# A four-layer fp32 trunk on one core: the SSD's row broadcasts, the transposed head outputs and the chain of the closing norm

## The chip, the core and the metric

The kernel runs on one core of one Trainium2 chip. The metric is the device time of one execution in microseconds (us). The engines are the matrix engine (PE, with its weight loads), DVE and POOL (vector work), ACT (scalar functions) and SP, whose queue issues the weight transfers.

## The reference

```python
for layer in range(2):
    h = rms_norm(x, g[0])
    if layer % 2 == 0:   # combined projection, then two mixers
        mix = concat(gla_mixer(...), na_mixer(...)) @ even_w_out
    else:
        mix = concat(ssd_mixer(...), swa_mixer(...)) @ odd_w_out
    x = x + rms_norm(mix, g[1])
    h = rms_norm(x, g[2])
    f = (silu(h @ ffn_w_gate[layer]) * (h @ ffn_w_up[layer])) @ ffn_w_down[layer]
    x = x + rms_norm(f, g[3])
```

There are 256 tokens of width 2048, all in float32. `rms_norm` divides by the root of the mean square and multiplies with a gain per column. The SSD has 16 heads of 64 columns in two groups, run in both directions:

```python
seg  = a_cum[l] - a_cum[m]              # per head, masked to one side
y    = (exp(seg) * (C B^T)) @ (x * dt)  # both directions added
y    = (y + x * d_skip) * silu(z)
out  = rms_norm(y, norm_g)              # over 1024 columns
```

Beside it stands a windowed attention (SWA) of 8 heads.

## The kernel before, in words

Weights stream from memory in halves of 512 KB (`load_half`, SP's queue). Each half is split into a rounded part `whi` (a CAST on ACT, L198) and a rest `wlo` (a subtraction on DVE, L200); each tile of a product then takes three matmuls of 512 columns (L226, L227, L228, here called main matmuls). Two of the FFN's products use the triples at L694 to L696. A program of pieces written by hand fixes the order at the ends of the layers, and a planner with simulated times places the rest.

Small work (convolutions, heads of the mixers) runs as generators beside the main matmuls: `tick` adds `rate` per tile of work, `step` advances the first `width` generators by one yield each. In the odd mixer these are RATE1 and WIDTH1 (L45).

**The end of a layer.** `post` takes the last product in four column blocks n = 0 to 3, for two halves of the tokens t = 0, 1. Each block is added to `f` on DVE (`add`, L444), squared and summed on ACT (`sumsq`, L360), and multiplied in place with the gains `gb` (L484: POOL for n < 2, DVE else), which must wait until ACT has read the block. At n = 3 `rstd` (L345 ff.) adds the four sums (L351), scales them and adds EPS (L355) on DVE, and POOL takes the power -0.5 (L356, result `prs`). Then the string PROG[0] (L54) orders the pieces: X0 to X3 add the four blocks to `x` (L468, DVE), T transposes a block of the new x on PE (L342, four matmuls `tp`), G makes its rounded part on ACT (L385), L the rest on DVE (L389), `p` prepares one half of weights (CAST and `wlo`), `q` issues a held back half of the last products. Capitals are t = 0, small letters t = 1. Pieces are pinned: PE and DVE keep this order. X is also saved to memory from POOL's queue (L1389). In the last layer there is no T; X is written out by SP (the tail).

**The SSD, before.** `ssd_dt` makes the cumulated decays `ac` (48 rows, both directions) and splits them into a rounded part and a rest (`achl`). For each head `ssd` broadcasts the head's two rows to 128 partitions with a matmul with a selecting column (`acb`, L1293), subtracts the transposed decays (`seg`, L1298, DVE, four pieces), takes the exponential on ACT, and multiplies with dt and with C B^T on POOL and DVE (L1305 to L1314 are POOL's). Four matmuls (eight records, 64 columns each) give `yp` with tokens on the partitions (L1320). POOL's x times `dskip` is added, the result is gated with `sz`, squared and summed on ACT; at the end ACT scales y, 16 transposes turn it and `split` makes the two parts for the output product.

Of the kernel before, what the change touches and what calls it, by code (L numbers as in the profile page):

```python
# [44 lines left out]
RATE1, WIDTH1 = .9, 6  # L45
# [8 lines left out]
PROG = ("X0 X1 p X2 p p X3 T0 q G0 T1 q q G1 L0 T2 p L1 p T3 G2 q x0 L2 x1 p G3 x2 x3 L3",  # L54
# [7 lines left out]
           ("alog", (1,)), ("dskip", (16,)), ("sink", (8,)), ("snT", (8,))),  # L62
# [31 lines left out]
class Trunk:  # L94
# [263 lines left out]
    def sumsq(self, src, acc):  # L358
        j = self.junk.tile([P, 512], mybir.dt.bfloat16, tag="junk", name=self.nm("sq"))
        self.nc.scalar.activation(j, src, AF.Square, accum_out=acc)  # L360
# [47 lines left out]
    def post(self, li, gi, nseg, after, f=None, before=None):  # L408
# [7 lines left out]
        rs = [self.small([P, 1], "prs", "prs") for _ in range(2)]  # L416
        state = {"si": 0}
# [7 lines left out]
        def seg(mk, xk):  # L425
# [25 lines left out]
            def run(prog):  # L451

                for c in prog.split():
# [12 lines left out]
                    xs, d = self.x[t][j // 2][:, s2], f[t][j // 2][:, s2]  # L466
# [5 lines left out]
            for n in range(4):  # L472
                def evac(t, ps, n=n):
# [5 lines left out]
                    with self.tc.high_priority(offset=NORM):  # L479
                        d = add(t, ps, n, n == 3)  # L480
                        self.sumsq(d, ssp[t][:, n:n + 1])
                        if n == 3:
                            self.rstd(ssp[t], 4, D, rs[t])
                        i = (nc.gpsimd if n < 2 else nc.vector).tensor_mul(out=d, in0=d, in1=gb[n])  # L484
                        if n == 3:
                            self.pin(i)
# [600 lines left out]
    def odd_mixers(self, norm, after):  # L1087
        nc = self.nc
        self.have = {}
# [24 lines left out]
        ssp = [self.small([P, 2], "yss", "yss") for _ in range(2)]  # L1114
        for g in range(2):
# [4 lines left out]
            xs = self.slot([P, 2, 512], nm="xs")  # L1120
            self.have[f"xs{g}"] = xs
            for c in range(4):
                self.conv(4 * g + c, xt, row, self.conv_end_x(xs, c, f"xs{g}{c}"))
# [51 lines left out]
    def conv_end_x(self, xs, c, key):  # L1175
        nc = self.nc

        def end(y):
            nc.vector.scalar_tensor_tensor(out=y[:, 1], in0=y[:, 1], scalar=1.0, in1=y[:, 0], op0=ALU.add, op1=ALU.mult)
            ps = self.mx([P, 2, P], "xsT")  # L1180
            for t in range(2):
                nc.tensor.transpose(ps[:, t], y[:, 1, t * P:(t + 1) * P], self.ident)
            nc.scalar.mul(xs[:, :, c * P:(c + 1) * P], ps, 0.5)
# [4 lines left out]
    def ssd_dt(self, xu):  # L1188
# [35 lines left out]
        hl = self.slot([P, 2, T], F32R, nm="achl")  # L1224
        zero = self.mtmp([P, 2, T], nm="dz")
        nc.vector.memset(zero, 0.0)
        nc.scalar.copy(hl, zero)
        for d in range(2):
            a = ac[32 * d:32 * d + 16]
            nc.scalar.copy(hl[0:16, d], a)  # L1230
            hb = zero[32 * d:32 * d + 16, 0]
            if d:
                nc.vector.tensor_copy(hb, hl[0:16, d].bitcast(F32))
            else:
                hb = hl[0:16, d].bitcast(F32)
            nc.vector.tensor_sub(hl[32:48, d], a, hb)
# [7 lines left out]
        sel = self.keep.tile([P, 16], F32R, tag="sel", bufs=1, name="sel")  # L1244
        nc.scalar.copy(sel, zero[:, 1, 0:16])
        for d in range(2):
            r = slice(32 * d, 32 * d + 16)
            nc.scalar.copy(sel[r], self.ident[r, r])
        self.have["dt"] = (hl, nat, sel)
        yield  # L1250

# [17 lines left out]
    def ssd(self, g, bc, ssp):  # L1269

        nc = self.nc
        yield from self.need("dt", f"bc{g}0", f"bc{g}1")
        hl, nat, sel = self.have["dt"]
        cb = self.ssd_cb(bc)
        cbf = cb.rearrange("p a b -> p (a b)")
        xs = self.have[f"xs{g}"]
# [4 lines left out]
        for qd in range(2):  # L1281
            yield from self.need(f"xs{g}{2 * qd}", f"xs{g}{2 * qd + 1}")
            cols = slice(256 * qd, 256 * qd + 256)
            xd = self.mtmp([P, 2, 4, 64], nm="xd")
            dk = self.dskip[:, 8 * g + 4 * qd:8 * g + 4 * qd + 4]
            for t in range(2):
                nc.gpsimd.tensor_mul(out=xd[:, t], in0=xs[:, t, cols].rearrange("p (h c) -> p h c", h=4),
                                     in1=dk.unsqueeze(2).broadcast_to([P, 4, 64]))
            yp = self.mx([P, 2, 256], "yp")
            for hq in range(4):  # L1290
                h, hc = 8 * g + 4 * qd + hq, (4 * qd + hq) * 64
                pb = self.mx([P, 2, T], "acb")
                nc.tensor.matmul(pb.rearrange("p a t -> p (a t)"), sel[:, h:h + 1].to_broadcast([P, P]),  # L1293
                                 hl.rearrange("p a t -> p (a t)"), start=True, stop=True)
# [7 lines left out]
                for i, (c0, c1, d, l0, mt) in enumerate(parts):  # L1302
                    r = 32 * d + h
                    if i in PSTT:
                        nc.gpsimd.tensor_scalar(out=s[:, c0:c1], in0=s[:, c0:c1], scalar1=nat[:, 2 + mt, r:r + 1],  # L1305
                                                scalar2=None, op0=ALU.mult)
                        if i == PSTT[-1]:
# [7 lines left out]
                if PY:  # L1315
                    yield
                for lt in range(2):
                    o = yp[:, lt, hq * 64:(hq + 1) * 64]
                    for mt in range(2):
                        nc.tensor.matmul(o, sb[:, lt + 4 * mt], xs[:, mt, hc:hc + 64], start=mt == 0, stop=mt == 1)  # L1320
                yield
            if y is None:
                y = self.slot([P, 2, 512], nm="y")
# [9 lines left out]
    def ssd_out(self, ssp, mix):  # L1333
# [3 lines left out]
        for g in range(2):  # L1337
            self.new_mix(mix, g)
# [147 lines left out]
```

## Time and profile before

| | us |
|---|---|
| three runs | 2190.62, 2187.39, 2187.41 |
| median | 2187.41 |
| profiled execution | 2186.18 |
| its span, first to last instruction | 2184.4 |

The mean clock granted to PE was 0.998 of full speed. The page gives busy times for each engine, DVE 1732.4 us, ACT 1219.6 and POOL 170.7 among them. Rows of a timeline give the start of a group of instructions in us from the span's start, its length, and in brackets the idle time of the engine ahead of it and what ended it. Records of PE overlap: the end of a record is modelled, so distances between starts are read.

### The profile page before, as it was taken

Reading aid. Unit: us, or ns where it says so; the run is one execution under the profiler, and the core shown is the slowest. Engines: PE = TensorE matmul, PEld = TensorE weight load, DVE = VectorE, ACT = ScalarE, POOL = GpSimd, SP = SyncE. Lnnn points to the kernel's source line nnn. Section 1 sums busy time; section 2 is a strip of 40 time slices with the busy share of each in tenths; the row PEclk is TensorE's granted clock in tenths of the full one; section 3 lists DMA queues with packets and bytes.
Section 4 is the critical chain, followed back from the end, with each engine's and each line's share of the span. In section 5 each row is a group of like instructions: output and inputs, shape, how many; then the busy total and the mean of one; then the engine's idle time right before and its main releaser. Section 6 shows DMA issues by size and latency. Waiting matters only on the chain. (4 is left out here: it accounts for less than half of the span.)

```text
span 2184.4 us, 28289 instructions
## 1 busy us (share of the span) xinstructions
PE 2154.6 (99%) x10416; PEld 1801.2 (82%) x10416; DVE 1732.4 (79%) x2208; ACT 1219.6 (56%) x1619; POOL 170.7 (8%) x217
## 2 busy tenths in 40 slices
PE   8999999999999999999999999999999999999997
PEld 7888888788888888888879988778888888888886
DVE  6988655766878898888879997776787889888786
ACT  7645445555565555555556455655556555555653
POOL 0001110100000000000021363210000000000001
PEclk9999999999999999999999999999999999999999
DMA  8444565674675655567466443567466555646644
GB/s 293 147 136 161 191 196 192 198 274 143 201 238 180 206 169 200 190 208 250 159 219 227 155 155 128 200 203 273 147 198 230 192 205 167 213 166 221 242 154 144
DMA packets 117322, 424.49 MB, mean 194 GB/s; under 512 B 13392, under 2 KB 13520, under 8 KB 117184
## 3 DMA queue, kind: packets, MB, share of 16 engines
q1 hardware_dynamic: 110592, 400.61, 54.6%
q0 software_dynamic: 6448, 21.99, 3.0%
q8 instruction: 81, 1.33, 0.2%
q14 instruction: 57, 0.47, 0.1%
q10 hardware_dynamic: 144, 0.10, 0.0%
HBM read 414.25 MB, written 8.39 MB: 193 GB/s over the span
## 5 line engine op out<-in xcount | busy, mean ns | idle before, releaser
L200 DVE TENSOR_TENSOR wlo<-raw,whi 128x1024 fp32r<-128x1024 f32 x608 | 750.1, 1239 | 291.9 <-ACT whi L198 283.2
L198 ACT CAST whi<-raw 128x1024 fp32r<-128x1024 f32 x608 | 639.2, 1054 | 591.7 <-PE acc L228 397.9
L228 PE MATMUL acc<-whi,xt 128*128 128x512 f32 x1760 | 686.9, 391 | 0.0
L227 PE MATMUL acc<-wlo,xt 128*128 128x512 f32 x1760 | 686.0, 391 | 0.2 <-DVE wlo L200 0.2
L226 PE MATMUL acc<-whi,xt 128*128 128x512 f32 x1760 | 675.8, 391 | 1.3 <-ACT xt L385 1.3
L226 PEld LDWEIGHTS acc<-whi,xt 128*128 128x128 f32 x1760 | 330.8, 188 | 69.4 <-ACT xt L385 1.7
L227 PEld LDWEIGHTS acc<-wlo,xt 128*128 128x128 f32 x1760 | 330.8, 188 | 69.2 <-DVE wlo L200 0.7
L228 PEld LDWEIGHTS acc<-whi,xt 128*128 128x128 f32 x1760 | 330.7, 188 | 68.2
L198 ACT CAST whi<-sw 128x1024 fp32r<-128x1024 f32 x252 | 265.7, 1054 | 207.6 <-PE acc L228 141.1
L200 DVE TENSOR_TENSOR wlo<-sw,whi 128x1024 fp32r<-128x1024 f32 x252 | 305.2, 1219 | 55.6 <-ACT whi L198 52.4
L696 PE MATMUL sq<-whi,so 128*128 128x512 f32 x504 | 196.1, 389 | 0.0
L695 PE MATMUL sq<-wlo,so 128*128 128x512 f32 x504 | 196.1, 389 | 0.0
L694 PE MATMUL sq<-whi,so 128*128 128x512 f32 x504 | 195.8, 390 | 0.0
L643 DVE TENSOR_TENSOR sw<-sw,sw 128x1024 f32<-128x1024 f32 x144 | 174.2, 1218 | 14.4 <-DMA sw<-sstream 13.8
L259 PE MATMUL acc<-xt,whi 128*128 128x512 f32 x384 | 136.3, 400 | 0.0
L696 PEld LDWEIGHTS sq<-whi,so 128*128 128x128 f32 x504 | 94.6, 188 | 19.7
L695 PEld LDWEIGHTS sq<-wlo,so 128*128 128x128 f32 x504 | 94.6, 188 | 19.4
L694 PEld LDWEIGHTS sq<-whi,so 128*128 128x128 f32 x504 | 94.6, 188 | 19.4
L262 PE MATMUL acc<-xt,wlo 128*128 128x256 f32 x384 | 105.0, 284 | 0.0
L434 POOL DMA_DIRECT2D gb<-norm_gains x16 | 8.7, 545 | 1196.1 <-issue 1183.1
L226 PE MATMUL acc<-whi,mixh 128*128 128x512 f32 x256 | 98.4, 396 | 0.0
L228 PE MATMUL acc<-whi,mixl 128*128 128x512 f32 x256 | 97.9, 391 | 0.0
(272 smaller groups left out, 2324.4 us busy)
## 6 DMA issues: line engine op xcount, KB each, us to landing
raw<-wstream SPq DMA_DIRECT2D x612, 512.0 KB, 4.9
sw<-sstream SPq DMA_DIRECT2D x144, 512.0 KB, 6.6
gb<-norm_gains POOLq DMA_DIRECT2D x16, 256.0 KB, 4.4
xm<-x POOLq DMA_DIRECT2D x16, 256.0 KB, 4.5
x<-xm POOLq DMA_DIRECT2D x8, 512.0 KB, 5.6
x<-x SPq DMA_DIRECT2D x4, 512.0 KB, 8.5
x<-x POOLq DMA_DIRECT2D x4, 512.0 KB, 5.7
xf<-x POOLq DMA_DIRECT2D x8, 256.0 KB, 3.5
```

The costliest lines, as they stand in the source:

```text
L198: self.pin(nc.scalar.copy(hi, src))
L200: self.pin(nc.vector.tensor_sub(lo, src, hi.bitcast(F32)))
L226: self.pin(nc.tensor.matmul(ps[t], xh, wh[:, k % 2], start=s, stop=False))
L227: self.pin(nc.tensor.matmul(ps[t], xh, wl[:, k % 2], start=False, stop=False))
L228: self.pin(nc.tensor.matmul(ps[t], xl, wh[:, k % 2], start=False, stop=e))
L259: wide = lambda s, e: nc.tensor.matmul(ps, wh[:, kt % 8], self.joined(kt, xt), start=s, stop=e)
L262: nc.tensor.matmul(ps[:, 0], wl[:, kt % 8], xt[0][kt // 4][:, kt % 4, :], start=False, stop=False)
L434: self.tc.keep_in_program_order(nc.gpsimd.dma_start(out=gb[n], in_=self.dr["norm_gains"][li, gi, n * 512:(n + 1) * 512].partition_broadcas ...
L643: nc.vector.tensor_add(a, a, b)
L694: nc.tensor.matmul(ps, xh, wh[:, k], start=s, stop=False)
L695: nc.tensor.matmul(ps, xh, wl[:, k], start=False, stop=False)
L696: nc.tensor.matmul(ps, xl, wh[:, k], start=False, stop=e)
```

## The change

Three things change together.

1. The norm at a layer's end. The squares are scaled, so that their sums add up to the mean. At n = 2 DVE adds the first three sums and EPS; at n = 3 ACT adds the last one itself (Identity with a bias), and POOL takes the power of that. The product with the gains of n = 3 goes to a tile of its own, `pg`, so that it need not wait for the square; that of t = 1, n = 1 moves from POOL to DVE.
2. The order of pieces, PROG[0]: two `p` stand ahead of X2 X3, all four X ahead of T0; L0, G2 and the pieces of t = 1 stand elsewhere. WIDTH1 goes from 6 to 7.
3. The SSD. POOL writes the decays to memory (`acrows`) and reads each pair's rows back to all 128 partitions (512 KB for a pair of heads); the `acb` matmuls, the split of `ac` and the selecting columns go. `yp` is made transposed for a pair of heads: x is the stationary part (64 columns), `seg` streams with 256 columns, and the two heads' outputs lie on partitions 0 to 63 and 64 to 127. The D-skip is one operation on DVE with x transposed; `z` is transposed for the gate (16 transposes); the squares are summed over partitions by matmuls with ones (`yss`); and the factor of the norm is applied from a row that `rstd_rows` spreads.

```diff
-RATE1, WIDTH1 = .9, 6
+RATE1, WIDTH1 = .9, 7
...
-PROG = ("X0 X1 p X2 p p X3 T0 q G0 T1 q q G1 L0 T2 p L1 p T3 G2 q x0 L2 x1 p G3 x2 x3 L3",
+PROG = ("X0 X1 p p X2 X3 p T0 q G0 T1 q q G1 T2 p L0 L1 q p T3 G2 L2 x0 G3 x1 p x2 x3 L3",
...
-        self.nc.scalar.activation(j, src, AF.Square, accum_out=acc)
+        self.nc.scalar.activation(j, src, AF.Square, scale=scale, accum_out=acc)
...
-                    xs, d = self.x[t][j // 2][:, s2], f[t][j // 2][:, s2]
+                    xs, d = self.x[t][j // 2][:, s2], prod[t][j]
...
-                        self.sumsq(d, ssp[t][:, n:n + 1])
+                        self.sumsq(d, ssp[t][:, n:n + 1], D ** -0.5)
+                        if n == 2:
+                            nc.vector.reduce_sum(out=rs[t], in_=ssp[t][:, 0:3], axis=AX.X)
+                            nc.vector.tensor_scalar_add(rs[t], rs[t], EPS)
                         if n == 3:
-                            self.rstd(ssp[t], 4, D, rs[t])
-                        i = (nc.gpsimd if n < 2 else nc.vector).tensor_mul(out=d, in0=d, in1=gb[n])
+                            nc.scalar.activation(ssp[t][:, 3:4], ssp[t][:, 3:4], AF.Identity, bias=rs[t])
+                            nc.gpsimd.tensor_tensor(out=rs[t], in0=ssp[t][:, 3:4], in1=self.mhalf, op=ALU.pow)
+                        p = prod[t][n] = d if n < 3 else self.tmp([P, 512], nm="pg")
+                        i = (nc.gpsimd if n < 2 - t else nc.vector).tensor_mul(out=p, in0=d, in1=gb[n])
...
+        rows = self.dram.tile([16, 2, T], F32, name="acrows")
         for d in range(2):
...
+            nc.gpsimd.dma_start(out=rows[:, d], in_=ac[32 * d:32 * d + 16])
...
+    def ac_rows(self, k):
+
+        if k in self.acs or k > 7:
+            return
+        self.acs[k] = self.slot([P, 2, 2, T], nm="acb")
+        self.tc.keep_in_program_order(self.nc.gpsimd.dma_start(
+            out=self.acs[k], in_=self.have["dt"][0][2 * k:2 * k + 2].partition_broadcast(P)))
...
-            for hq in range(4):
-                h, hc = 8 * g + 4 * qd + hq, (4 * qd + hq) * 64
-                pb = self.mx([P, 2, T], "acb")
-                nc.tensor.matmul(pb.rearrange("p a t -> p (a t)"), sel[:, h:h + 1].to_broadcast([P, P]),
-                                 hl.rearrange("p a t -> p (a t)"), start=True, stop=True)
+        for c in range(4):
+            yield from self.need(f"xs{g}{c}")
+            self.ac_rows(4 * g + c)
+            self.ac_rows(4 * g + c + 1)
+            both = []
+            for i in range(2):
+                h = 8 * g + 2 * c + i
+                pb = self.acs[4 * g + c][:, i]
...
-                if PY:
-                    yield
-                for lt in range(2):
-                    o = yp[:, lt, hq * 64:(hq + 1) * 64]
-                    for mt in range(2):
-                        nc.tensor.matmul(o, sb[:, lt + 4 * mt], xs[:, mt, hc:hc + 64], start=mt == 0, stop=mt == 1)
+                both.append(s)
                 yield
+            if PY:
+                yield
+            yp = self.mx([P, T], "yp")
+            for mt in range(2):
+                for i in range(2):
+                    r = slice(64 * i, 64 * i + 64)
+                    self.turn(nc.tensor.matmul(yp[r], xs[:, mt, c * P + 64 * i:c * P + 64 * i + 64],
+                                               both[i][:, 512 * mt:512 * mt + T], start=mt == 0, stop=mt == 1), i or mt)
+            yield
...
-            nc.vector.tensor_add(y[:, :, cols], yp, xd.rearrange("p t h c -> p t (h c)"))
+            nc.vector.scalar_tensor_tensor(out=y[:, c], in0=xT[:, c], scalar=self.dskip[:, 4 * g + c:4 * g + c + 1],
+                                           in1=yp, op0=ALU.mult, op1=ALU.add)
...
+                    nc.tensor.transpose(tp[:, k, t * P:(t + 1) * P], z[:, t, c:c + P], self.ident)
+            nc.vector.tensor_mul(y[:, cs], y[:, cs], tp)
+            nc.scalar.activation(sq[:, cs], y[:, cs], AF.Square)
...
+        nc.vector.tensor_add(sq[:, 0:2], sq[:, 0:2], sq[:, 2:4])
+        ps = self.mx([P, 2], "yss")
         for t in range(2):
...
+            for c in range(2):
+                nc.tensor.matmul(ps[:, t:t + 1], sq[:, c, t * P:(t + 1) * P], self.ones[:, 0:1], start=c == 0, stop=c == 1)
+        nc.vector.tensor_copy(ssp[:, :, g], ps)
...
+        row = self.rstd_rows(rs)
...
-                nc.scalar.mul(y[:, t], y[:, t], r)
...
-                tp = self.transpose4(self.have[f"y{g}"][:, t])
-                self.split(tp, mix[0][g][:, :, sl], mix[1][g][:, :, sl], self.snT[:, 4 * g:4 * g + 4], self.mtmp)
...
+                    nc.vector.scalar_tensor_tensor(out=y[:, c], in0=y[:, c], scalar=self.snT[:, 4 * g + c:4 * g + c + 1],
+                                                   in1=row, op0=ALU.mult, op1=ALU.mult)
+                nc.scalar.copy(mix[0][g][:, cs], y[:, cs])
+                nc.vector.tensor_sub(mix[1][g][:, cs], y[:, cs], mix[0][g][:, cs].bitcast(F32))
```

The changed kernel's lines stand 1 to 18 lower (X at L469, the product with the gains at L490, Identity at L487, the power at L488, `yp` at L1318).

PE in the odd mixer, before: `yp` of two heads and the broadcasts of two more, between main matmuls.

```order
L228 MATMUL acc_11296<-whi_11495,xt_9664 128x512
L226 MATMUL acc_11296<-whi_11495,xt_9664 128x512
L1320 MATMUL yp_11092<-xs_10152,seg_11095 128x64 x4
L1320 MATMUL yp_10968<-xs_10654,seg_11103 128x64 x4
L1293 MATMUL acb_11198<-achl_10127,sel 128x512
L1293 MATMUL acb_11206<-achl_10127,sel 128x512
L227 MATMUL acc_11296<-wlo_11497,xt_9664 128x512
L228 MATMUL acc_11296<-whi_11495,xt_9664 128x512
```

PE in the odd mixer, after: one pair of heads, its first matmul apart from the other three.

```order
L228 MATMUL acc_11129<-whi_11158,xt_9679 128x512
L1318 MATMUL yp_11207<-seg_11034,xs_10141 64x256
L226 MATMUL acc_11265<-whi_11255,xt_9588 128x512
L227 MATMUL acc_11265<-wlo_11257,xt_9588 128x512
L1318 MATMUL yp_11207<-seg_11118,xs_10141 64x256
L1318 MATMUL yp_11207<-seg_11034,xs_10141 64x256
L1318 MATMUL yp_11207<-seg_11118,xs_10141 64x256
L228 MATMUL acc_11265<-whi_11255,xt_9588 128x512
L226 MATMUL acc_11265<-whi_11255,xt_9588 128x512
```

The broadcasts are gone, and a `yp` row is one matmul of 64 output partitions and 256 columns; of the eight pairs four stand like this one, with main matmuls between, and four stand with their four rows together.

ACT at the end of layer 0's mixer, before (`sq` the squares, `pss_3030` the sums of t = 0).

```order
L198 CAST whi_3773<-raw_3706 128x1024
L360 ACTIVATE sq_3743,pss_3031<-f_3264 128x512
L360 ACTIVATE sq_3778,pss_3030<-f_3348 128x512
L198 CAST whi_3809<-raw_3746 128x1024
L198 CAST whi_3817<-raw_3752 128x1024
L360 ACTIVATE sq_3800,pss_3031<-f_3264 128x512
L385 ACTIVATE xt_3829<-tp_3832,ca 128x128 x4
L198 CAST whi_3823<-raw_3771 128x1024
```

ACT at the same place, after; L487 is the new Identity.

```order
L198 CAST whi_3775<-raw_3706 128x1024
L360 ACTIVATE sq_3745,pss_3031<-f_3264 128x512
L360 ACTIVATE sq_3780,pss_3030<-f_3348 128x512
L198 CAST whi_3809<-raw_3748 128x1024
L487 ACTIVATE pss_3030<-pss_3030,prs_3032 128x1
L198 CAST whi_3815<-raw_3754 128x1024
L360 ACTIVATE sq_3800,pss_3031<-f_3264 128x512
L385 ACTIVATE xt_3829<-tp_3832,ca 128x128 x4
```

The Identity comes behind the last square of t = 0, with one CAST between.

DVE at the same place, before (L444 add, L468 X, L351 and L355 the norm, L200 `wlo`).

```order
L351 TENSOR_REDUCE ss_3780<-pss_3030 128x1
L484 TENSOR_TENSOR f_3348<-f_3348,gb_3612 128x512
L355 TENSOR_SCALAR ms_3782<-ss_3780 128x1
L444 TENSOR_TENSOR f_3264<-f_3264,acc_3786 128x512
L468 SCALAR_TENSOR_TENSOR x_3598<-f_3095,prs_3032,x_3598 128x512 x2
L200 TENSOR_TENSOR wlo_3811<-raw_3746,whi_3809 128x1024
L468 SCALAR_TENSOR_TENSOR x_3600<-f_3348,prs_3032,x_3600 128x512
L200 TENSOR_TENSOR wlo_3819<-raw_3752,whi_3817 128x1024
L200 TENSOR_TENSOR wlo_3825<-raw_3771,whi_3823 128x1024
L468 SCALAR_TENSOR_TENSOR x_3600<-f_3348,prs_3032,x_3600 128x512
L389 SCALAR_TENSOR_TENSOR xt_3829<-tp_3832,ca,xt_3829 128x128 x4
```

DVE at the same place, after (L445 add, L469 X, L490 product with the gains).

```order
L445 TENSOR_TENSOR f_3348<-f_3348,acc_3760 128x512
L490 TENSOR_TENSOR pg_3784<-f_3348,gb_3612 128x512
L445 TENSOR_TENSOR f_3264<-f_3264,acc_3786 128x512
L469 SCALAR_TENSOR_TENSOR x_3598<-f_3095,prs_3032,x_3598 128x512 x2
L200 TENSOR_TENSOR wlo_3811<-raw_3748,whi_3809 128x1024
L200 TENSOR_TENSOR wlo_3817<-raw_3754,whi_3815 128x1024
L469 SCALAR_TENSOR_TENSOR x_3600<-f_3348,prs_3032,x_3600 128x512
L469 SCALAR_TENSOR_TENSOR x_3600<-pg_3784,prs_3032,x_3600 128x512
L490 TENSOR_TENSOR f_3264<-f_3264,gb_3608 128x512
L200 TENSOR_TENSOR wlo_3827<-raw_3773,whi_3825 128x1024
```

The sum and the scaling are gone from here, X2 and X3 stand together behind two `wlo`, and a product that POOL did (`gb_3608`, t = 1) stands behind X3.

## Rows read from the trace of the kernel before

**Rows 1.** the page, part 1: busy time, share of the span, instructions.

```profile
PE 2154.6 (99%) x10416; PEld 1801.2 (82%) x10416; DVE 1732.4 (79%) x2208; ACT 1219.6 (56%) x1619; POOL 170.7 (8%) x217
```

**Rows 2.** PE's waits by line: total us, times, longest us.

```profile
PE tp L342 <- DVE x L468: 5.9, 6, 1.4
...
PE tp L342 <- issue: 3.0, 2, 1.5
PE apo L1062 <- DVE mxv L1031: 1.6, 1, 1.6
...
PE apo L1062 <- ACT pT L1058: 0.8, 1, 0.8
...
PE yp L1320 <- POOL seg L1314: 0.2, 1, 0.2
```

**Rows 3.** PE's timeline: start us, us, engine line op; one `acb` broadcast.

```profile
1319.46 0.40 PE L1293 MATMUL acb<-achl,sel 128*128 128x512 f32 x1
1319.69 0.40 PE L228 MATMUL acc<-whi,xt 128*128 128x512 f32 x1
```

**Rows 4.** PE's timeline: one head's `yp` and the matmuls behind it.

```profile
1387.86 1.00 PE L1320 MATMUL yp<-xs,seg 128*128 128x64 f32 x8
...
1388.98 0.40 PE L228 MATMUL acc<-whi,mixl 128*128 128x512 f32 x1
```

**Rows 5.** PE's timeline: `gs` (split rows), then `as` (256 columns).

```profile
79.34 0.39 PE L259 MATMUL acc<-xt,whi 128*128 128x512 f32 x1
79.66 1.16 PE L895 MATMUL gs<-ge 64*128 64x128 f32 x16
...
80.98 0.39 PE L259 MATMUL acc<-xt,whi 128*128 128x512 f32 x1
...
1361.36 1.02 PE L1029 MATMUL as<-kw,qT 128*128 128x256 f32 x4
...
1362.45 0.40 PE L228 MATMUL acc<-whi,xt 128*128 128x512 f32 x1
```

**Rows 6.** PE's timeline at the end of layer 0's mixer.

```profile
420.56 0.39 PE L228 MATMUL acc<-whi,mixl 128*128 128x512 f32 x1
422.39 0.66 PE L342 MATMUL tp<-ca,x 128*128 128x128 f32 x4 [1.45 <-DVE x L468]
...
429.31 0.66 PE L342 MATMUL tp<-ca,x 128*128 128x128 f32 x4 [1.25 <-DVE x L468]
```

**Rows 7.** DVE's timeline at the same place.

```profile
420.98 0.69 DVE L444 TENSOR_TENSOR f<-f,acc 128x512 f32<-128x512 f32 x1 [0.34 <-PE acc L228]
421.59 1.41 DVE L468 SCALAR_TENSOR_TENSOR x<-f,prs,x 128x512 f32<-128x512 f32 x2
422.91 2.75 DVE L200 TENSOR_TENSOR wlo<-raw,whi 128x1024 fp32r<-128x1024 f32 x1
...
428.52 0.74 DVE L468 SCALAR_TENSOR_TENSOR x<-f,prs,x 128x512 f32<-128x512 f32 x1
```

**Rows 8.** ACT's timeline at the same place.

```profile
419.67 1.03 ACT L198 CAST whi<-raw 128x1024 fp32r<-128x1024 f32 x1
```

**Rows 9.** POOL's timeline at the same place.

```profile
420.72 0.57 POOL L356 TENSOR_TENSOR prs<-ms,mhalf 128x1 f32<-128x1 f32 x1 [1.30 <-DVE ms L355]
...
423.26 1.30 POOL L484 TENSOR_TENSOR f<-f,gb 128x512 f32<-128x512 f32 x1
```

**Rows 10.** DVE's timeline at the end of layer 1's mixer.

```profile
1459.82 1.22 DVE L200 TENSOR_TENSOR wlo<-raw,whi 128x1024 fp32r<-128x1024 f32 x1
```

**Rows 11.** DVE's timeline in the tail, then POOL's.

```profile
2168.36 3.77 DVE L468 SCALAR_TENSOR_TENSOR x<-f,prs,x 128x512 f32<-128x512 f32 x4
...
2177.20 2.74 DVE L468 SCALAR_TENSOR_TENSOR x<-f,prs,x 128x512 f32<-128x512 f32 x4 [0.66 <-POOL prs L356]
...
2169.34 1.57 POOL L484 TENSOR_TENSOR f<-f,gb 128x512 f32<-128x512 f32 x1 [1.29 <-ACT sq L360]
```

**Rows 12.** POOL's groups by line and form: busy us, mean ns.

```profile
L1314 POOL TENSOR_TENSOR seg<-seg 128x256 f32<-128x256 f32 x16 | 20.4, 1282 | 0.6
```

## What the change was predicted to do

> **What bounds the kernel now.** I read the page's list of busy times first: the matrix engine (PE) is busy for 2154.6 of 2184.4 us [rows 1], so time can come only from what PE executes, from the places where it waits, and from the tail after its last matmul. Next the list of PE's waits: little is in it, and the reader should see that it has two families [rows 2]. One is `tp`, the transposes at a layer's end that wait for the new `x`: 5.9 us in six waits on DVE and 3.0 in two put down to issue. The other is the odd mixer: `apo` of the windowed attention on DVE (1.6) and ACT (0.8), `yp` of the SSD on POOL (0.2). Last I read the timelines of the places that the diff touches, PE first, then the engine it waits for. Because PE's records overlap, a price on PE is a distance between starts: one main matmul of 512 columns costs 0.23 [rows 3].
>
> **The change, part by part.** The profiled execution took 2186.2 us, 1.2 less than the median of 2187.4; I make the sum against the first and add 1.2.
>
> *Broadcasts.* The 16 `acb` matmuls leave PE. One costs the distance 1319.46 to 1319.69, 0.23 [rows 3], so -3.7. In their place POOL issues two small writes and eight reads of 512 KB. I cost these at nothing: each read is issued one pair of heads ahead, and the cover is the work of that pair. If the cover is gone, `seg` comes late (third rival).
>
> *Head outputs.* Before, a head costs 1387.86 to 1388.98 less one main matmul, 0.89 [rows 4]; 16 heads, -14.2. After, a pair of heads takes four matmuls, two for each half of the output partitions, eight records of 256 columns. Four such records in `as` cost 1361.36 to 1362.45 less 0.23, 0.86, so 0.215 each [rows 5]. Do two halves run side by side? No row of before splits the output partitions. The nearest are the `gs` records, which split the contraction rows: 16 records of 128 columns, with one L262 of 256 columns (0.115) behind them, fill 79.34 to 80.98 less 0.23, so 1.29 without the L262 [rows 5]. At half of 0.215 each, 16 in a row would be 1.72; eight side by side are 0.86, and 0.43 is left over, which I read as a toll for going into split mode and back. So an undisturbed pair of heads is 4 x 0.215 + 0.43 = 1.29. The order shows four of the eight pairs undisturbed and four with main matmuls between the first half and the other three. For these I add one lone matmul and a second toll, 0.43 + 0.43, giving about 2.15. Sum 4 x 1.29 + 4 x 2.15 = 13.8. The bounds: 8.6 (no toll anywhere, 8 x 0.86 + 4 x 0.43) and 19.0 (nothing side by side: 8 x 1.72, a toll for each of 12 visits).
>
> The Trainium skill (TensorEngine Tiling (Array Packing), Key Properties) speaks against this part: it says that a change of tiling mode drains the engine, which would make the split groups pay twice; the 0.43 above agrees with it. By TensorE: Matmul & The Clock Gate, Part 3, small outputs in different column groups run concurrently, with next to nothing per tile; by that alone the groups would cost the lower bound. No run here shows column halves yet.
>
> *Norm of y.* The 16 transposes of y become 16 of z, same shape: zero. Added are 16 records of one column (`yss`), priced at 0.11 each as `yp`'s 64-column records are (0.89 / 8) [rows 4], 1.8, and four for `rstd_rows`, 0.4. Bounds 1.0 to 2.6. The edits on DVE and ACT (gate, D-skip, the 0.5 folded away, fewer scalings) I cost at nothing, since PE has main matmuls beside them; if that cover fails, it shows as `apo` or `yp` waiting.
>
> PE's work in the SSD thus changes by -3.7 - 14.2 + 13.8 + 2.2 = **-1.9**, between -8.3 and +3.7.
>
> *Waits of the odd mixer.* They hold 2.6 [rows 2]. In the new order 15 main matmuls stand between a transpose `apt` and its `apo`, and `yp` waits only once for a pair. I take 1.0 as left: **-1.6**. Bounds -2.6 and +3 (each pair waits 0.4, as the larger yp gaps of before).
>
> *Layer ends.* Three boundaries share the 8.9 us of `tp` waits [rows 2]; the first (mixer to FFN of layer 0) stands for them. There T0 waits 1.45 and T3 1.25 [rows 6]. Is the first wait shortened? The norm's own chain gets shorter, but on ACT a CAST of 1.03 stands between the last square and the new Identity (the order), as it stood behind the square before [rows 8]; so Identity ends near 420.9 and POOL's pow (0.57 [rows 9]) near 421.5. On DVE the add of the other half stands ahead of X0, till 421.67, and X0 begins at 421.59 now [rows 7]. Both limits hold the first wait where it is. The later ones shrink: before, X2 and X3 stood among three `wlo`, X3 started at 428.52, and one of the `wlo` took 2.75 beside POOL's gain product [rows 7, 9], where one took 1.22 without it [rows 10]. After, that product moves to DVE (0.69, after X3), and X0 X1, two `wlo`, X2 X3 end near 421.6 + 1.4 + 2.4 + 1.4 = 426.8, 2.5 us before T3 could start. The first waits, 3 x 1.47 = 4.4, stay; the other 4.5 I take down to 1.5, because pieces that came early now make the `lo` pieces and `wlo` late: **-3.0**. Bounds -4.5 and 0.
>
> WIDTH1 lets one more background strand advance at once; I cost it at nothing beyond the order already counted. SP's queue of weight loads is the same row for row, and POOL's saves of `xm` come with their X, with one product less ahead of them: nothing.
>
> *Tail.* At the end no CAST stands behind the square. X of the second half of the tokens starts at 2177.20 [rows 11]. Before it, the first half's four X took 3.77, with POOL's product at 2169.34 beside them for 1.57 [rows 11]; without it they take 2.75 as the last four do, 1.0 less; the product moves to DVE, into its idle time before the last add. On the norm's chain the sum, the scale and the gain product no longer stand behind the last square: some 0.8 less on DVE, 0.1 more on ACT. **-1.7**, bounds 0 and -2.5.
>
> Sum: -1.9 - 1.6 - 3.0 - 1.7 = -8.2; 2186.2 - 8.2 + 1.2 = **2179.2 us**.
>
> **Rivals.** 0.2% of the time, 4.4 us, is about what a measurement of this kernel can tell from no change.
>
> *Halves in turn.* If the two column halves don't run side by side, the pairs cost 19.0 in place of 13.8: 2184.4. Against it: the `gs` rows. For it: those split rows, not columns.
>
> *No toll.* If going into column halves costs nothing, 8.6 in place of 13.8: 2174.0. For it: the 0.43 is one sample of a group beside small shapes.
>
> *SSD late, the slower side.* The subtraction that makes `seg` reads its rows from SBUF now, where it read PSUM, and POOL works on `seg` too. POOL's add of 256 columns takes 1.28 on average [rows 12], and the `wlo` of 2.75 shows what DVE and POOL do to each other [rows 7, 9]. If every pair's `yp` waits for one such add, PE loses 8 x 1.28 = 10.2, and the 1.6 of the mixer's waits is not won: 2179.2 + 11.8 = 2191.0. It decides from the point at which a pair's last add ends after PE has come to its `yp`, about one add late at each. Against it: of 16 heads, `yp` waited 0.2 us in all on POOL [rows 2]. The Trainium skill (SBUF — State Buffer, 🔬 SBUF: two separate sides) has this as a rule: DVE in its fast modes from SBUF and POOL share a port pair as a lock, and descriptors of POOL's DMAs wait too. The 2.75 agrees for two SBUF inputs; for the DMA issues no row here decides.
>
> That the change doesn't do what it says can be in one part: the first waits stay, as said, so the norm's shorter chain wins only in the tail. This lies in the forecast.
>
> **How the numbers follow.** Forecast 0.56, halves in turn 0.13, no toll 0.18, SSD late 0.13. The forecast's own bounds on waits and tail are some 4 us each way, 2175 to 2183. The range adds the no-toll case with part of its spread and halves in turn: 2172 to 2187; what it leaves out is SSD late and the far ends. Faster means under 2183.0: no toll, nine tenths of the forecast and a quarter of halves in turn, 0.71. Slower is over 2191.8: under half of SSD late and nothing else of weight, so with its doubled form 0.08. The rest, 0.21, is the same.
>
> **What would show it.** Right: `yp` pairs at 1.3 undisturbed and 2.1 split; no `acb` on PE; the first `tp` wait near 1.5 at each boundary and the later ones near 0.5; X of the second half near 2175.5. Wrong: `yp` or DVE's `seg` waiting for POOL or for a DMA at most pairs, pairs of 1.7 or more undisturbed, a first `tp` wait under 1 us, or new waits of main matmuls for `wlo` at the boundaries.

## The result, and the profile after

The changed kernel takes 2174.74 us (median of six runs, 2174.09 to 2176.83) against 2187.4 for the kernel before in the same comparison: the ratio is 0.9941, with a 95% interval of 0.9928 to 0.9954. It is 12.7 us faster, where 8.2 were forecast; 2179.2 was said and the range was 2172 to 2187. The profiled execution took 2174.74 with a span of 2172.9.

The page's busy times and PE's list of waits, of the changed kernel:

```profile
PE 2151.1 (99%) x10356; PEld 1790.2 (82%) x10356; DVE 1729.1 (80%) x2223; ACT 1216.7 (56%) x1613; POOL 169.5 (8%) x215
```

```profile
PE tp L342 <- DMA ca<-ca: 5.1, 1, 5.1
PE tp L342 <- issue: 3.0, 2, 1.5
PE tp L342 <- DVE x L469: 1.4, 1, 1.4
PE acc L226 <- ACT xt L385: 1.4, 1, 1.4
PE acc L228 <- DVE xt L389: 0.4, 2, 0.2
```

Against [rows 1, 2] the reader should see that PE's busy time fell by only 3.5 us; most of the gain is in waits. Of the `tp` waits at the layer ends only the three first ones are left (3.0 + 1.4; the 5.1 for `ca` stood there before as well, 5.2), and `apo` and `yp` no longer appear in the list at all.

The main matmuls are the same 9320 records in both traces, so the place where time is won can be read from their starts: the k-th one after less the k-th one before, the change from one place to the next.

| stretch | before, from to | won in the two traces | forecast |
|---|---|---|---|
| layer 0's mixer | 0 to 420 | -0.6 | 0 |
| its end | 420 to 500 | 1.4 | 1.0 |
| FFN 0 | 500 to 1131 | 0.3 | 0 |
| FFN 0's end | 1131 to 1200 | 1.4 | 1.0 |
| odd mixer | 1200 to 1440 | 6.8 | 3.5 |
| its end | 1456 to 1490 | 0.9 | 1.0 |
| tail, behind the start of the last main matmul | 2172.8 to 2184.4 | 1.2 | 1.7 |

Together the two traces differ by 11.4; the medians differ by 12.7, because the profiled execution before lies 1.2 under its median. (The 0.6 in layer 0, where nothing is changed, is of the size by which single executions differ there; the profiled executions of two experiments, product on POOL and late head first, stood some 3 us behind the changed kernel there, with a wait of `gs` for DVE.)

PE's timeline of the changed kernel, an undisturbed pair of heads and then a split one:

```profile
1294.01 0.39 PE L226 MATMUL acc<-whi,xt 128*128 128x512 f32 x1
1294.33 1.08 PE L1318 MATMUL yp<-seg,xs 128*64 128x256 f32 x8
1295.34 0.50 PE L227 MATMUL acc<-wlo,xt 128*128 128x512 f32 x1
1295.68 0.40 PE L228 MATMUL acc<-whi,xt 128*128 128x512 f32 x1
```

```profile
1269.46 0.39 PE L228 MATMUL acc<-whi,xt 128*128 128x512 f32 x1
1269.78 0.65 PE L1318 MATMUL yp<-seg,xs 128*64 128x256 f32 x2
1270.35 0.50 PE L226 MATMUL acc<-whi,xt 128*128 128x512 f32 x1
1270.69 0.40 PE L227 MATMUL acc<-wlo,xt 128*128 128x512 f32 x1
1271.02 1.08 PE L1318 MATMUL yp<-seg,xs 128*64 128x256 f32 x6
1272.02 0.50 PE L228 MATMUL acc<-whi,xt 128*128 128x512 f32 x1
1272.36 0.40 PE L226 MATMUL acc<-whi,xt 128*128 128x512 f32 x1
```

With the main matmuls around them taken off (two of 0.227 each time), the undisturbed pair costs 1.22 (1294.01 to 1295.68), a lone first matmul 0.78 (1269.46 to 1270.69), and the three others 1.22. Before, two heads cost 1.78 [rows 4].

DVE's, ACT's and POOL's timelines at the end of layer 0's mixer, after:

```profile
421.57 0.69 DVE L445 TENSOR_TENSOR f<-f,acc 128x512 f32<-128x512 f32 x1 [1.02 <-PE acc L228]
422.18 1.41 DVE L469 SCALAR_TENSOR_TENSOR x<-f,prs,x 128x512 f32<-128x512 f32 x2
423.50 2.36 DVE L200 TENSOR_TENSOR wlo<-raw,whi 128x1024 fp32r<-128x1024 f32 x2
425.77 0.74 DVE L469 SCALAR_TENSOR_TENSOR x<-f,prs,x 128x512 f32<-128x512 f32 x1
426.44 0.74 DVE L469 SCALAR_TENSOR_TENSOR x<-pg,prs,x 128x512 f32<-128x512 f32 x1
```

```profile
420.27 1.03 ACT L198 CAST whi<-raw 128x1024 fp32r<-128x1024 f32 x1
421.20 0.29 ACT L487 ACTIVATE pss<-pss,prs 128x1 f32<-128x1 f32 x1
```

```profile
421.57 0.57 POOL L488 TENSOR_TENSOR prs<-pss,mhalf 128x1 f32<-128x1 f32 x1 [1.56 <-ACT pss L487]
```

Identity stands behind a CAST, the power ends at 422.14, the add ends at 422.26, and X0 starts at 422.18: both limits are there, as forecast from [rows 7 to 9]. The two `wlo` take 2.36 together where one took 2.75 beside POOL's product [rows 7], and X3 ends at 427.2 in place of 429.3.

The tail, DVE:

```profile
2165.44 2.08 DVE L469 SCALAR_TENSOR_TENSOR x<-f,prs,x 128x512 f32<-128x512 f32 x3 [1.08 <-POOL prs L488]
```

The X of the second half of the tokens start 2.9 us behind the last main matmul's start (2162.53), where they started 4.4 behind it before [rows 11].

### The profile page after: what moved, and what is told of

The parts are those of the page before. It is cut to its first block, busy times and chain, and to the rows that moved or that the text cites. A ratio compares the mean times of both kernels' runs of the same rounds, so it can differ in the third digit from the quotient of the medians.

```text
span 2172.9 us, 28179 instructions
## 1 busy us (share of the span) xinstructions
PE 2151.1 (99%) x10356; PEld 1790.2 (82%) x10356; DVE 1729.1 (80%) x2223; ACT 1216.7 (56%) x1613; POOL 169.5 (8%) x215
## 4 chain that ended last, share of the span: by engine, by line
PE 78%; issue 1%; DVE 1%; POOL 0%; ACT 0%; POOLq 0%; DVEq 0%; ACTq 0%
PE acc L228 19%; PE acc L227 19%; PE acc L226 18%; PE sq L701 5%; PE sq L700 5%; PE sq L702 5%; PE tp L342 1%; PE accb L299 1%; PE accb L300 1%; PE accb L301 1%; PE yp L1318 0%; DVE x L469 0%; PE apo L1068 0%; PE as L1035 0%; PE accl L280 0%
## 5 line engine op out<-in xcount | busy, mean ns | idle before, releaser
L200 DVE TENSOR_TENSOR wlo<-raw,whi 128x1024 fp32r<-128x1024 f32 x608 | 745.3, 1232 | 288.6 <-ACT whi L198 280.2
L200 DVE TENSOR_TENSOR wlo<-sw,whi 128x1024 fp32r<-128x1024 f32 x252 | 305.4, 1221 | 55.6 <-ACT whi L198 52.6
```

The source lines that it names most:

```text
L200: self.pin(nc.vector.tensor_sub(lo, src, hi.bitcast(F32)))
```

## The experiments

Each run is named, with its median of five runs or more; the changed kernel's is 2174.74, and that of the kernel before was 2187.27, 2187.60 and 2186.96 in the three comparisons.

### The layer ends

**Old pieces** (2177.78, 2177.25 to 2178.89).

```diff
-PROG = ("X0 X1 p p X2 X3 p T0 q G0 T1 q q G1 T2 p L0 L1 q p T3 G2 L2 x0 G3 x1 p x2 x3 L3",
+PROG = ("X0 X1 p X2 p p X3 T0 q G0 T1 q q G1 L0 T2 p L1 p T3 G2 q x0 L2 x1 p G3 x2 x3 L3",
```

> The changed kernel with the old order of pieces at the layer ends (PROG[0]), all else as changed. Theory A: the order carries most of what the layer ends won (some 4 us in the traces), so 2.5 to 3.5 us slower than the changed kernel, about 2177.7, and T3 waits near 1 us again. Rival B: the norm's chain and the product taken from POOL carry it; then within 0.7 us of the changed kernel, about 2175.2.

3.0 slower, as theory A has it: later `tp` waits return at all three ends (`tp` on DVE 7.1 us in seven waits). The order of the pieces is worth 3.0 beside the new norm.

**Old norm** (2180.94, 2179.44 to 2181.04).

```diff
-                            nc.scalar.activation(ssp[t][:, 3:4], ssp[t][:, 3:4], AF.Identity, bias=rs[t])
-                            nc.gpsimd.tensor_tensor(out=rs[t], in0=ssp[t][:, 3:4], in1=self.mhalf, op=ALU.pow)
-                        p = prod[t][n] = d if n < 3 else self.tmp([P, 512], nm="pg")
-                        i = (nc.gpsimd if n < 2 - t else nc.vector).tensor_mul(out=p, in0=d, in1=gb[n])
+                            self.rstd(ssp[t], 4, D, rs[t])
+                        i = (nc.gpsimd if n < 2 else nc.vector).tensor_mul(out=d, in0=d, in1=gb[n])
```

> The changed kernel with the old norm at the layer ends (sum, scale and gain product of the last block in the chain, POOL's product at t = 1), the new order of pieces kept. Theory A: the first waits stay near 1.6 each, the tail is 1.3 longer and the layer ends lose under 1 us, so about 2176.7. Rival B: the shorter chain is what lets X2 and X3 end early; then 3 us or more slower, 2178 and up, with new waits of tp at all three ends.

6.2 slower, so theory A is wrong in size and B right about it; but B's waits of `tp` are not there. DVE's and PE's timelines at the end of layer 0's mixer, of this run:

```profile
424.18 3.88 DVE L200 TENSOR_TENSOR wlo<-raw,whi 128x1024 fp32r<-128x1024 f32 x2
427.99 1.40 DVE L468 SCALAR_TENSOR_TENSOR x<-f,prs,x 128x512 f32<-128x512 f32 x2
...
437.28 0.16 DVE L351 TENSOR_REDUCE ss<-pss 128x1 f32<-128x4 f32 x1 [1.75 <-ACT sq L360]
```

```profile
432.57 0.50 PE L228 MATMUL acc<-whi,xt 128*128 128x512 f32 x1 [0.85 <-DVE xt L389]
...
439.49 0.50 PE L228 MATMUL acc<-whi,xt 128*128 128x512 f32 x1 [1.17 <-DVE xt L389]
```

X2 and X3 are late because two `wlo` take 3.88, and PE then waits 0.85 with a main matmul for a `lo` piece of t = 0. The second wait, 1.17, has another cause: the old sum (L351) of t = 1 stands in DVE's order ahead of a `wlo` and the `lo` pieces, and DVE stands idle for 1.75 until ACT has squared the last block. The first wait stays at 1.4 to 1.5, as the forecast said.

**Product on POOL** (2177.06, 2176.11 to 2179.44). One part of the norm undone:

```diff
-                        i = (nc.gpsimd if n < 2 - t else nc.vector).tensor_mul(out=p, in0=d, in1=gb[n])
+                        i = (nc.gpsimd if n < 2 else nc.vector).tensor_mul(out=p, in0=d, in1=gb[n])
```

> The changed kernel with one thing of the norm undone: the gain product of t = 1, n = 1 goes back from DVE to POOL. With the whole old norm the kernel was 6.2 us slower, and two wlo took 3.88 beside POOL's product where they take 2.36 in the changed kernel. Theory A: that product is what makes X2 and X3 late (1.5 at each layer end), the rest of the 6.2 is the tail and the later prs of t = 1; so 2 to 3 us slower than the changed kernel, about 2177.2, with waits of main matmuls for xt at the ends of the layers. Rival B: the chain of sum, scale and product did it; then within 0.7 us, about 2175.0.

2.3 slower, as theory A has it, with waits of main matmuls for `xt` (1.8 us in three) in the profile. The profiled execution is the slowest of the five, 2179.44, and 3.1 of that lies in layer 0; at the layer ends it loses 1.6 against the changed kernel by the starts. With the old norm the layer ends lose 4.4 by the starts and the tail 1.2 (the other 0.7 of that trace lies in layer 0, where nothing differs). So of the 4.4 some 1.6 is the product beside `wlo`, and the rest, some 2.8, stays with the old chain; the 1.17 behind DVE's idle 1.75 is one part of it, and the others were not taken apart.

**Identity first** (2182.88, 2181.77 to 2184.08). The next CAST is ordered behind each Identity:

```diff
-                            nc.scalar.activation(ssp[t][:, 3:4], ssp[t][:, 3:4], AF.Identity, bias=rs[t])
+                            i = nc.scalar.activation(ssp[t][:, 3:4], ssp[t][:, 3:4], AF.Identity, bias=rs[t])
+                            self.before_cast = i.ins.name
...
+            if self.before_cast:
+                self.tc.add_manual_dep(i.ins, self.before_cast, mybir.DependencyInfo(
+                    mybir.DependencyClass.NoSync, mybir.DependencyReason.DATA), reason="order")
+                self.before_cast = None
```

> The changed kernel with the next CAST on ACT ordered behind the new Identity (a dependency of order alone); on DVE X0 and X1 then stand ahead of the last add of the other half. Theory A: the two limits named in the prediction hold the first wait at 1.6: the CAST ahead of the Identity and the add ahead of X0. With both gone X0 starts about 0.9 sooner at each of the three layer ends: 2.6 us faster, about 2172.1, first waits near 0.7. Rival B: something else holds it (the power on POOL, or the add that is late now and the square behind it); then within 0.7 us of the changed kernel.

Theory A's mechanism is shown and its gain is not there. PE's timeline:

```profile
422.19 0.65 PE L347 MATMUL tp<-ca,x 128*128 128x128 f32 x4 [0.64 <-DVE x L474]
...
438.16 0.50 PE L233 MATMUL acc<-whi,xt 128*128 128x512 f32 x1 [1.66 <-DVE xt L394]
```

The first wait is 0.64 here and 0.68 and 0.67 at the other two ends, 0.8 less each (1.45 and twice 1.49 in the changed kernel). The two limits were lifted together, so which of them holds was not separated. But in the second half of the tokens the CASTs now stand behind the Identity, DVE stands idle for 0.78 until one is through and `wlo` can start, and PE waits 1.66 for the `lo` piece behind it. And the schedule that is worked out from the new order puts a `yp` earlier in the mixer, where the pair waits 3.6 us for POOL; behind that the granted clock is 0.50 for 3.4 us. By the starts the layer ends lose 3.1 against the changed kernel, and the mixer 4.2.

**Identity first, t = 0 only** (2174.99, 2174.05 to 2175.57).

```diff
-                            self.before_cast = i.ins.name
+                            self.before_cast = None if t else i.ins.name
```

> The Identity ahead of the next CAST for the first half of the tokens only. With it for both halves the first waits fell from 1.6 to 0.6 at all three layer ends, but in the second half two wlo came late behind CASTs (1.6 us of waits at two ends), and the order of the odd mixer shifted (4 us). Theory A: with the second half and the mixer's order as in the changed kernel, 1.0 at each end is won and some 0.5 of it lost again where DVE is late with the lo pieces: 1 to 2 us faster than the changed kernel, about 2173.2. Rival B: DVE works without a pause through the layer end, so what PE wins at T0 it waits for later; then within 0.7 us of 2174.7.

No faster: theory B. PE's waits of this run:

```profile
PE acc L233 <- DVE xt L394: 1.5, 4, 0.6
PE tp L347 <- PE acc L233: 1.4, 2, 0.7
...
PE acc L232 <- DVE wlo L205: 0.7, 2, 0.5
PE tp L347 <- DVE x L474: 0.6, 1, 0.6
```

The `tp` waits fell from 4.4 to 2.0, and those of main matmuls for DVE's `xt` and `wlo` rose from 0.6 to 2.2. By the starts the three layer ends win 3.8 over the kernel before, where the changed kernel wins 3.7. DVE works without a pause from X0 to the end of the first half in the changed kernel (421.57 to 436.9); a PE that starts sooner there waits later.

### The odd mixer

**SSD alone** (2184.09, 2182.57 to 2186.70, eleven runs): the changed kernel with the old norm and the old pieces as in the two runs above, and the old width.

```diff
-RATE1, WIDTH1 = .9, 7
+RATE1, WIDTH1 = .9, 6
```

> The kernel before with the SSD's part of the change alone (old norm, old order of pieces, WIDTH1 6). Theory A, by the starts of the main matmuls in the two traces: the odd mixer holds 6.4 us of the gain (2.7 less work on PE, 3.5 in waits of apo and yp), so about 2181.0, with the waits of the three layer ends and the tail as in the kernel before. Rival B, the forecast's smaller sum: 3.5 us, about 2183.9, the rest of the mixer's gain coming from WIDTH1 or from pieces that arrive earlier.

3.2 faster than before, ratio 0.9987 (0.9978 to 0.9995): by its size rival B. The eleven times fall into two groups, six from 2182.57 to 2184.09 and five from 2185.64 to 2186.70; the trace is one of the first group, and of the second there is none. Its trace has no wait of `apo` or `yp`, but a new one of 2.4 us, a main matmul for ACT's first copies of the output product.

**Width 6** (2178.21, 2177.69 to 2178.42): the changed kernel with the same one line.

> The changed kernel with WIDTH1 6 in place of 7. The run of the SSD's part alone (WIDTH1 6) was 4.5 us longer in the odd mixer than the changed kernel, 2.6 of it one wait of a main matmul for ACT's first copies of the output product. Theory A: the width brings it (the strands end later, and so does the copy); then about 4 us slower, 2178.7, with that wait in the profile. Rival B: it came with the shifted start of the old pieces; then within 0.7 us, about 2175.0.

3.5 slower, with that wait: theory A. PE's and ACT's timelines, and a stretch with the clock granted to PE (behind the busy times of the five engines; then the DMA engines' busy share and GB/s):

```profile
1374.77 1.07 PE L1335 MATMUL zT<-ca,sz 128*128 128x128 f32 x8
1378.27 0.50 PE L226 MATMUL acc<-whi,mixh 128*128 128x512 f32 x1 [2.42 <-ACT f L443]
...
1378.98 0.63 PE L228 MATMUL acc<-whi,mixl 128*128 128x512 f32 x1
1379.41 0.63 PE L226 MATMUL acc<-whi,mixh 128*128 128x512 f32 x1
```

```profile
1377.11 0.63 ACT L1337 ACTIVATE ysq<-y 128x512 f32<-128x512 f32 x1 [1.89 <-DVE y L1336]
1377.64 2.03 ACT L443 COPY f<-acc 128x512 f32<-128x512 f32 x4
```

```profile
1380.00:1382.00 2.00, 2.00 (x7) 1.51 (x6) 0.69 (x1) 0.21 (x1) 0.00 (x0) 0.50 0.04 12
```

The copy `f<-acc` at 1377.64 stands on ACT behind `ysq`, the square of the gated y, which waits for DVE and so for the transposes `zT` at 1374.77; PE can't begin the next product before the copy has emptied its bank, and waits 2.42. After that pause the granted clock is 0.50 (the lower level, 1.2 of 2.4 GHz): between 1378.98 and 1381.97 a main matmul costs 0.43 in place of 0.23. The same place in the changed kernel, with width 7:

```profile
1372.49 1.07 PE L1335 MATMUL zT<-ca,sz 128*128 128x128 f32 x8
1373.32 0.49 PE L226 MATMUL acc<-whi,mixh 128*128 128x512 f32 x1
```

From `zT` to the next main matmul it is 3.50 with width 6 and 0.83 with width 7, so the pause costs 2.7; the ten main matmuls behind it lose some 1.6 more by the clock. With width 7 `yss` and `zT` stand twelve main matmuls earlier in PE's order, the copies are through before their banks are wanted, and nothing waits.

**SSD with width 7** (2179.72, 2179.46 to 2180.08): the run of the SSD alone, with

```diff
-RATE1, WIDTH1 = .9, 6
+RATE1, WIDTH1 = .9, 7
```

> The SSD's part alone again, but with WIDTH1 7: the run with 6 took 2184.1. Theory A: the 2.4 us wait of a main matmul for ACT's copy of f, and some 1 us more, go with the width, as in the changed kernel: 3.5 us faster than that run, about 2180.6, no such wait in the profile. Rival B: the width is worth that only beside the new layer ends; then within 0.7 us of 2184.1.

4.4 faster than with 6: theory A (some 3.2 against the faster of the two groups of that run). There is no such wait in the profile. The mixer gains 6.8 in this trace, as in the changed kernel; the layer ends gain nothing.

**No SSD** (2188.11, 2183.64 to 2189.27, eleven runs): the changed norm, pieces and width on the old SSD.

```diff
-RATE1, WIDTH1 = .9, 6
+RATE1, WIDTH1 = .9, 7
...
-                            self.rstd(ssp[t], 4, D, rs[t])
+                            nc.scalar.activation(ssp[t][:, 3:4], ssp[t][:, 3:4], AF.Identity, bias=rs[t])
+                            nc.gpsimd.tensor_tensor(out=rs[t], in0=ssp[t][:, 3:4], in1=self.mhalf, op=ALU.pow)
```

> The changed kernel without the SSD's part (norm, pieces and WIDTH1 7 on the kernel before's SSD). Theory A: the layer ends and the tail won 5.5 us by the two traces (1.6, 1.7, 0.9 and 1.3), and the old SSD's waits stay: about 2182. Rival B: the width helps the old SSD too, by the 3.5 that it was worth in the changed kernel: about 2178.5.

Neither: no faster than before, ratio 1.0004 (0.9995 to 1.0013). Its layer ends win what they win in the changed kernel, but the mixer loses 6.4. PE's waits, and the stretches with the granted clock:

```profile
PE yp L1326 <- POOL seg L1320: 2.7, 2, 2.5
PE apt L1058 <- DVE sc L1051: 1.9, 1, 1.9
```

```profile
1367.00:1370.00 3.00, 0.63 (x5) 0.32 (x3) 2.34 (x7) 2.48 (x8) 2.84 (x4) 1.00 0.54 186
...
1375.00:1381.00 6.00, 5.96 (x16) 4.85 (x17) 1.01 (x3) 1.33 (x3) 0.00 (x0) 0.50 0.01 3
```

A `yp` waits for POOL and the attention's transposes for DVE; PE is busy for 0.63 of 3 us, and the `apo` behind run at 0.50. Ten of the eleven executions took 2187.47 to 2189.27, at a mean granted clock of 0.995 or 0.996, as the profiled one; one took 2183.64, at 0.999. So without the fall of the clock this kernel comes within 2 us of theory A, and some 4.5 us go with the fall; of the one execution no trace was kept. That the width does this, and not the 2 us by which the mixer starts sooner, was not separated.

**Late head first** (2173.62, 2172.92 to 2176.99):

```diff
-                for i in range(2):
+                for i in (1, 0):
...
-                                               both[i][:, 512 * mt:512 * mt + T], start=mt == 0, stop=mt == 1), i or mt)
+                                               both[i][:, 512 * mt:512 * mt + T], start=mt == 0, stop=mt == 1), mt or i == 0)
```

> The changed kernel with the four matmuls of a pair begun with the head whose seg is made last, so that the four stand together in all eight pairs (four were split). Theory A: a lone first matmul costs 0.78 in the changed kernel's trace, the other three 1.22, as much as an undisturbed group; so 4 x 0.78 = 3.1 us faster, about 2171.6. Rival B: the group now waits for its last seg, which the lone matmul hid; then within 0.7 us of the changed kernel, with waits of yp on POOL.

1.1 faster by the medians, within the spread of the runs: between the theories. The profiled execution is the slowest of the five, 2176.99, and 3.5 us of it lie in layer 0; its mixer is 1.2 shorter than the changed kernel's by the starts. All eight groups stand together at 1.22, but `yp` waits for its seg as B said (0.4), and the attention's transposes `rtp`, to which PE comes sooner, wait 1.2 for ACT and 0.3 for DVE.

**Halves in turn** (2177.01, 2176.27 to 2178.62):

```diff
-            for mt in range(2):
-                for i in range(2):
+            for i in range(2):
+                for mt in range(2):
```

> The changed kernel with the two column halves of a pair in turn (both matmuls of the first head, then both of the second). Theory A: halves in adjacent records run side by side (an undisturbed group takes 1.22 in the changed kernel's trace) and in turn they do not: 8 records of 0.215 and the toll, about 2.1, so some 0.9 more for a group; with the groups cut in two in four places about 5 us slower, 2180. Rival B: the records run fast whatever their order (the next record's weights being loaded is what counted); then within 1 us of the changed kernel.

2.3 slower, and 2.05 of it is one wait of `yp` for POOL. A group of both heads, and one head alone, in PE's timeline:

```profile
1223.34 1.09 PE L1318 MATMUL yp<-seg,xs 128*64 128x256 f32 x8
1224.37 0.38 PE L299 MATMUL accb<-xt,whi 128*128 128x256 f32 x1
```

```profile
1360.38 1.08 PE L1318 MATMUL yp<-seg,xs 128*64 128x256 f32 x4
1361.39 0.50 PE L227 MATMUL acc<-wlo,xt 128*128 128x512 f32 x1
```

Eight records take from 1223.34 to 1224.37, as long as four of one head alone (1360.38 to 1361.39). That the heads are queued one behind the other shows where main matmuls stand between: there it is four records of one head and then four of the other, at 1.22 each, where the changed kernel has two and six. So theory A's price falls: the halves run side by side though they stand in turn in the queue.

**Both improvements** (2173.36, 2172.59 to 2180.68): late head first and Identity first for t = 0.

```diff
-                for i in range(2):
+                for i in (1, 0):
...
+                            self.before_cast = None if t else i.ins.name
```

> The run before this one with the late head's matmul first in each pair as well. Theory A: the two add up; late first alone was 1.1 us faster than the changed kernel, so about 2172.1. Rival B: the earlier start of the mixer turns into waits of yp and rtp, as most of late first's 3.1 did; then no faster than the run before.

1.4 under the changed kernel by the medians, but one of five runs took 2180.68 (mean granted clock 0.995, where the others have 0.997 to 0.999), and its ratio to before, 0.9946 (0.9933 to 0.9958), is no better than the changed kernel's 0.9941. Its mixer, too, is 1.2 shorter than the changed kernel's by the starts, but no version was shown to beat the changed kernel in its time.

## Why the prediction was right, and where its sum was short

The forecast was 4.4 us too slow, inside its range. By the terms of its sum the traces won 2.7 (PE's work), 3.5 (waits of the mixer), 3.7 (layer ends) and 1.2 (tail), 11.1 of 11.4; 0.6 of the mixer's 6.8 is in none of these terms. The parts of the SSD (rows by DMA, transposed outputs, the norm) were run only together, so their shares are read from rows, and which of them took the `apo` waits away was not separated.

- **PE's work in the SSD** was forecast at -1.9. A pair costs 1.22 undisturbed (1.29 said) and 0.78 + 1.22 split (2.15 said), so 4 x 1.22 + 4 x 2.00 = 12.9 in place of 13.8; `yss` and `rb` cost 1.8 and 0.5, where 1.8 and 0.4 were said. It came to -2.7. The toll is 0.36, not 0.43.
- **Halves in turn** and **no toll** both fall: 8 records of 0.215, two at a time, are 0.86, and 1.22 is measured. That the time, 2174.74, lies beside the 2174.0 of "no toll" is chance: the toll is there, and what came on top of the forecast came from the other terms. The Trainium skill (TensorE: Matmul & The Clock Gate, Part 3: Packing small matmuls) has small outputs in different column groups run concurrently. The 1.22 agrees with it. The Trainium skill (the same section) also has matmuls start and end strictly in their order. The run with the halves in turn differs there: in order its eight records would take at least 1.5 without any toll, an estimate from this trace (the second head could begin when three records of 0.215 are through, and takes 0.86).
- **The waits of the odd mixer** were mis-sized: -1.6 said, of 2.6. By starts the waits before were 3.5, because the list of waits leaves out the smallest waits and what PE takes to resume, and all of it went.
- **WIDTH1 at nothing** is the step that failed. With the new SSD, width 6 has a new wait of 2.4 and a slow clock behind it, 4.3 together; width 7 removes them, which is worth 4.4 on the SSD alone and 3.5 in the changed kernel. The sum does not suffer by it, and that is luck: it left out both the new wait and what takes it away. Without the width the SSD wins 3.2 (2.3 in the mixer of its trace), near the 3.5 said for the mixer, again by luck: there what the sum lacks on one side (0.8 on PE, 1.9 of waits) stands against the 4.3.
- **The layer ends** were forecast at -3.0 and won 3.7. The first waits stayed, by both limits, as said; the later ones went nearly whole, where 1.5 was kept. That the product beside `wlo` costs 1.5 was read rightly from [rows 7, 9, 10]; the run that puts it back loses 2.3 (1.6 at the layer ends by its trace).
- **The tail**: -1.7 said, -1.2 measured.
- **SSD late**, the slower side, did not come: with the changed kernel no `yp` waits for POOL or for a DMA. But it is near: in two variants with the new SSD `yp` waited for POOL for 2.05 (halves in turn) and 3.6 us (Identity first). The Trainium skill (SBUF — State Buffer, 🔬 SBUF: two separate sides) has a DVE operation with two SBUF inputs and a POOL operation that reads SBUF block each other. The trace agrees: two `wlo` take 3.88 beside POOL's product of 1.31, and 2.36 without it.
- The 1.2 added for the median before was not needed: after, profiled run and median are the same, so the sum by the traces was 2178.0.

## What to carry to other kernels

Where an engine works without a pause through a stretch (DVE at these layer ends), shortening the wait ahead of it won nothing here; the product taken off POOL, which slowed DVE, did win. A setting that only reorders small work is to be costed by what stands behind that work on each in-order queue: one square ahead of four copies on ACT was worth 4 us here. The parts of such a change don't add up (undone one at a time they cost 3.0, 6.2 and 3.5, and without its SSD the rest wins nothing by the median), so each is to be tried with the others in place.

## What the runs showed that I had not expected

- Two heads' matmuls on separate halves of the output partitions ran side by side though all of one head's stood ahead of the other's: eight records in the time of four, 1.22.
- A pause of 2.4 us, with little work of PE ahead of it (`yss` and `zT`), was followed by 3 us at a granted clock of 0.50; the clock thus added some 1.6 to a price of 2.7. It fell so behind the `yp` waits of "Identity first" (2.63 and 1.01) as well, but not behind the single `yp` wait of 2.05 in "halves in turn", where it stayed at 1.00.
